# A hybrid RWKV-7 and attention layer: the next block's x fetched and normalised during the running block, and one matrix per chunk and head in the scan

## The chip, the cores and the metric

The kernel runs on one core of one Trainium2 chip. The metric is the device time of one execution in microseconds (us). One execution was also taken by the hardware profiler, which gives the trace that the rows below come from. Engines are named as in the profile: PE (TensorE, matmuls), PEld (its weight loads), DVE (VectorE), ACT (ScalarE), POOL (GpSimd), SP (SyncE, which issues DMAs). Times inside the trace are counted from the start of its span.

## What is computed

One layer on x (2048 tokens of 1024, float32) with three residual steps and a final norm. Half of the first step's width is a recurrent mixer, half a differential attention:

```python
proj = rms_norm(h, norm_mix_w[l]) @ w_in[l]
p_rwkv, p_diff = proj[..., :RWKV_COLS], proj[..., RWKV_COLS:]
h = h + jnp.concatenate([y_rwkv, y_diff], axis=-1) @ w_out[l]
h = h + memory_cross_attn(rms_norm(h, norm_mem_w[l]), rms_norm(mem, norm_src_w[l]), ...)
h = h + jnp.square(jax.nn.relu(hn @ w_up[l])) @ w_down[l]

def step(state, inp):                      # the recurrence, for each of 8 heads of 64
    r_t, w_t, k_t, v_t, kk_t, a_t = inp
    sa = jnp.einsum("bhvk,bhk->bhv", state, -kk_t)
    state = (state * w_t[:, :, None, :] + sa[..., None] * (kk_t * a_t)[:, :, None, :]
             + v_t[..., None] * k_t[:, :, None, :])
    y = jnp.einsum("bhvk,bhk->bhv", state, r_t)
    return state, y
```

The kernel does the recurrence in chunks of 64 tokens: inside a chunk everything is matrix products and the inverse of a triangular matrix, and only a 64x64 state per head goes from chunk to chunk.

## The kernel before

It has two phases. **Phase 1** (0 to about 1424 us) computes the projection `x @ w_in`, the recurrent mixer, the memory's keys and values, and the product with `w_out`. **Phase 2** (the rest: attention queries, memory attention, MLP) is the same in both kernels.

Phase 1 goes over four blocks of 512 tokens. Its backbone is `inproj_stream`, a row of items; an item is one 128x512 output tile made by 24 matmuls (three for each of 8 k-slices, a float32 product split in high and low parts: L631, L632, L634) into a PSUM ring `ps_acc` of two buffers. Its weight pieces come by SP, ACT makes the high part (L615) and POOL the low part (L616). The items' order is lead (2 items), keys, receptances and values of a unit (`rkv`), and `diff` items (q, k, v of the attention half) for each block; after the four blocks come memory items, "fold" items and the `w_out` items (L718 to L738). These matmuls are called the stream.

A unit is one block and one group of four heads (two pairs of heads); there are 8, numbered 0 to 7. Beside the stream each unit goes through a chain: features (`rwkv_features`; its first matmul is L291), scores (`ps_sc`, L359), the transposed scores (`ps_bt` L375, `ps_aT` L384, the latter in 64x64 tiles on the diagonal), the inverse (DVE, with DRAM round trips), the merge (`rwkv_merge`: `psz`, `psr2`, then L500 multiplies the inverse into the matrix `A`), the scan (`rwkv_scan`) and the output (`rwkv_out`). `run()` emits stream matmuls up to a given position, then a step of the unit's generator, and so on: `prep(u+1)` and `finish(u)` run beside each other, both under a raised priority (`urgent`), and the tile scheduler decides from this, from priorities and from its own idea of when data is there, which instruction comes next on each engine. PE takes its instructions in that fixed order.

In the scan a chunk of one pair takes four products of two heads each: L524 (`psu`, from `A` and the column block `UV`, which holds state and v), L526 (`psy`, from `AR`), then, when ACT has copied `psu` into `UV` (L528) and scaled the old state (L521), L534 (`pss`, the new state) and L536 (`psy`, the second part). DVE makes the next state from `pss` (L542). A float32 matmul shows as two records in the trace.

At the start of blocks 1 to 3 the lead item calls `prep_x`: it loads x again by 8 DMAs, transposes it (32 transposes of 128x128, L247), stores the transposed x, multiplies by the norm and splits high and low part; the buffers `xhi` and `xlo` have one copy each. At the start of the memory items `prep_mem` does the same for the memory tokens. At the end of phase 1, `first_queries` puts the first attention queries among the last stream items.

## Time and profile before

| | |
|---|---|
| time, median of 3 runs | 3764.45 us (3763.79 to 3769.11) |
| the profiled execution | 3768.81 us, its span 3767.1 us |
| PE busy | 3581.6 us, 95% |
| DVE, ACT, POOL busy | 1957.9, 1720.5, 1464.5 us |
| mean granted clock of PE | 0.968 |

The page puts 95% of the span as PE busy. A matmul's record covers its way through the array, so that records in a row overlap, and a short matmul that stands alone counts as busy for longer than it holds the next one up. The distance from the start of one record to the start of the next is therefore what the prediction goes by, not the mean length. The granted clock is 1.0 at 2.4 GHz and 0.5 at 1.2 GHz; a value between is a mean of stretches at either.

### The profile page before, as it was taken

The numbers are of one execution on the slowest core, as the hardware profiler recorded it, in microseconds if no ns is written. First come the engines' busy times: TensorE is split into PE (matmuls) and PEld (weight loads), VectorE is DVE, ScalarE is ACT, GpSimd is POOL, SyncE is SP. The second block draws the span as 40 slices with busy tenths as digits, with TensorE's granted clock in tenths as the row PEclk, the third lists the DMA queues.
The fourth block names the chain that finished last, engine by engine and source line by source line (L and its number), as shares of the span: only waits on it lengthen the run. The fifth ranks groups of instructions, "written<-read, shape, count | busy, mean of one in ns | idle before, by whom it ended". The sixth has DMA issues, their size and how long they took to land. (4 is left out here: it accounts for less than half of the span.)

```text
span 3767.1 us, 57886 instructions
## 1 busy us (share of the span) xinstructions
PE 3581.6 (95%) x21297; PEld 2871.5 (76%) x21297; DVE 1957.9 (52%) x4093; ACT 1720.5 (46%) x3802; POOL 1464.5 (39%) x1195
## 2 busy tenths in 40 slices
PE   7999999999999878899999989999999999999998
PEld 5767766767777767678787777888878888888887
DVE  4456666666574636465566756666634332313132
ACT  5364464454455626554455765555543421212123
POOL 4424324423434534344435435343353332222225
PEclk9989999999999899999999999999999999999999
DMA  4343342333335674343324425232243331111113
GB/s 149 107 128 88 82 127 84 86 107 88 87 88 160 207 210 142 106 121 93 113 79 118 139 73 144 79 112 78 85 152 94 111 102 48 48 51 48 48 57 108
DMA packets 566066, 390.52 MB, mean 104 GB/s; under 512 B 65187, under 2 KB 491254, under 8 KB 565782
## 3 DMA queue, kind: packets, MB, share of 16 engines
q1 hardware_dynamic: 534134, 329.55, 30.5%
q10 hardware_dynamic: 28064, 50.35, 4.0%
q0 software_dynamic: 3584, 6.92, 0.8%
q8 instruction: 168, 2.75, 0.3%
q14 instruction: 116, 0.95, 0.1%
HBM read 311.14 MB, written 75.56 MB: 103 GB/s over the span
## 5 line engine op out<-in xcount | busy, mean ns | idle before, releaser
L170 POOL TENSOR_TENSOR wlo<-wraw,whi 128x512 fp32r<-128x512 f32 x520 | 689.5, 1327 | 1247.6 <-ACT whi L169 1218.6
L616 POOL TENSOR_TENSOR wlo<-wraw,whi 128x512 fp32r<-128x512 f32 x288 | 413.8, 1438 | 597.4 <-ACT whi L615 479.3
L169 ACT ACTIVATE whi<-wraw 128x512 fp32r<-128x512 f32 x520 | 327.9, 631 | 639.9 <-PE ps_dn L187 327.0
L186 PE MATMUL ps_dn<-hdh,whi 128*128 128x512 f32 x1024 | 402.1, 393 | 2.3 <-DVE t L1408 1.2
L187 PE MATMUL ps_dn<-hdl,whi 128*128 128x512 f32 x1024 | 401.8, 393 | 0.3 <-DVE hdl L1413 0.3
L188 PE MATMUL ps_dn<-hdh,wlo 128*128 128x512 f32 x1024 | 398.8, 393 | 3.3 <-POOL wlo L170 3.1
L186 PE MATMUL ps_up<-h2h,whi 128*128 128x512 f32 x1024 | 400.1, 391 | 1.0 <-DVE t L1408 0.9
L187 PE MATMUL ps_up<-h2l,whi 128*128 128x512 f32 x1024 | 400.7, 391 | 0.0
L188 PE MATMUL ps_up<-h2h,wlo 128*128 128x512 f32 x1024 | 395.3, 391 | 0.8 <-POOL wlo L170 0.8
L631 PE MATMUL ps_acc<-xhi,whi 128*128 128x512 f32 x832 | 343.7, 414 | 20.0 <-ACT carry L278 18.9
L634 PE MATMUL ps_acc<-xhi,wlo 128*128 128x512 f32 x832 | 343.8, 414 | 2.2 <-POOL wlo L616 2.0
L632 PE MATMUL ps_acc<-xlo,whi 128*128 128x512 f32 x832 | 340.3, 409 | 0.0
L615 ACT ACTIVATE whi<-wraw 128x512 fp32r<-128x512 f32 x288 | 181.2, 630 | 273.4 <-PE ps_acc L632 98.0
L1422 DVE TENSOR_TENSOR ht<-ht,ps_dn 128x512 f32<-128x512 f32 x128 | 87.8, 686 | 347.3 <-PE ps_dn L188 347.2
L1048 ACT ACTIVATE pt<-ps_s,nmx 128x512 f32<-128x512 f32 (+3 forms) x320 | 198.4, 621 | 142.4 <-DVE nmx L1047 117.9
L1047 DVE TENSOR_REDUCE nmx<-ps_s 128x1 f32<-128x512 f32 (+3 forms) x320 | 192.5, 606 | 75.6 <-PE ps_s L1044 71.6
L188 PEld LDWEIGHTS ps_dn<-hdh,wlo 128*128 128x128 f32 x1024 | 193.1, 189 | 45.3 <-POOL wlo L170 6.4
L186 PEld LDWEIGHTS ps_dn<-hdh,whi 128*128 128x128 f32 x1024 | 193.0, 188 | 41.8 <-issue 1.6
L186 PEld LDWEIGHTS ps_up<-h2h,whi 128*128 128x128 f32 x1024 | 192.1, 188 | 41.3 <-DVE t L1408 1.6
L187 PEld LDWEIGHTS ps_dn<-hdl,whi 128*128 128x128 f32 x1024 | 193.2, 189 | 39.8 <-DVE hdl L1413 0.5
L188 PEld LDWEIGHTS ps_up<-h2h,wlo 128*128 128x128 f32 x1024 | 192.4, 188 | 40.3 <-POOL wlo L170 1.5
L187 PEld LDWEIGHTS ps_up<-h2l,whi 128*128 128x128 f32 x1024 | 192.3, 188 | 38.8
(336 smaller groups left out, 7772.4 us busy)
## 6 DMA issues: line engine op xcount, KB each, us to landing
wraw<-in_w_in_dram SPq DMA_DIRECT2D x208, 256.0 KB
wraw<-in_w_down_dram SPq DMA_DIRECT2D x208, 256.0 KB
wraw<-in_w_up_dram SPq DMA_DIRECT2D x192, 256.0 KB
s_hT<-xt ACTq DMA_DIRECT2D x64, 256.0 KB
wraw<-in_w_out_dram SPq DMA_DIRECT2D x56, 256.0 KB
s_qkvT<-qkv ACTq DMA_DIRECT2D x48, 256.0 KB
wraw<-in_w_mq_dram SPq DMA_DIRECT2D x48, 256.0 KB
wraw<-s_mb SPq DMA_DIRECT2D x48, 256.0 KB
```

The source lines that it names most:

```text
L169: nc.scalar.activation(out=hi, in_=raw, func=AF.Copy)
L170: nc.gpsimd.tensor_tensor(out=lo, in0=raw, in1=f32(hi), op=ALU.subtract)
L186: nc.tensor.matmul(ps, whi(k), ahi(k), start=(k == 0), stop=False)
L187: nc.tensor.matmul(ps, whi(k), alo(k), start=False, stop=False)
L188: nc.tensor.matmul(ps, wlo(k), ahi(k), start=False, stop=(k == nk - 1))
L615: nc.scalar.activation(out=hi, in_=raw, func=AF.Copy)
L616: nc.gpsimd.tensor_tensor(out=lo, in0=raw, in1=f32(hi), op=ALU.subtract)
L631: nc.tensor.matmul(o, hi[:, kk, :], xs[k][0], start=(k == 0), stop=False)
L632: nc.tensor.matmul(o, hi[:, kk, :], xs[k][1], start=False, stop=False)
L634: nc.tensor.matmul(o, lo[:, kk, :], xs[k][0], start=False, stop=last)
L1047: nc.vector.tensor_reduce(out=nmx[:, m, c:c + 1], in_=ps[:, 0:w], axis=AX.X, op=ALU.max, negate=True)
L1048: nc.scalar.activation(out=pt[:, cw(c)], in_=ps[:, 0:w], func=AF.Exp, bias=nmx[:, m, c:c + 1], accum_out=sm[:, m, c:c + 1])
```

## The change

Two things. First, `prep_x` is cut in two. `fetch_x` (load, transposes, store, norm) is a generator of 8 steps, run in front of the items m = 16 to 23 of the block before (one k-slice each), into eight new buffers `xn0` to `xn7`; `split_x` (8 high parts on ACT, 4 low parts on DVE, 4 on POOL) is what stays at the block's start. `prep_mem` moves in front of item m = 16 of block 3. The ring `xsl` has 2 buffers where it had 3. Second, the merge makes, for each chunk and head, one matrix `Q` of 128 rows and 128 columns whose product with the head's half of `UV` gives the chunk's new state before its decay and its y at once. The scan of a chunk and pair is then four matmuls in tiles 128x64 (L552) and two scaled copies on ACT; the merge has, for each half of a pair's chunks, 8 matmuls 64x128 (`psw2`, L512), one ACT copy, 16 matmuls 64x128 (`psm`, L520) and six additions on DVE. Scan work falls by 1024 + 512 (L500) matmuls, and 512 (L552) + 256 (`psw2`) + 512 (`psm`) come in. `y` is copied from PSUM by ACT before `rwkv_out`. Last, `dynamic_dma_scratch_size` is set to 2048. The merge's ten steps stand at 0.70 to 0.88 of a unit's stretch, the five of before at 0.72 to 0.88.

```diff
-def prep_x(g, pool, blk, rstd):
+def fetch_x(g, pool, blk, rstd):
...
     for k in range(KD):
-        xt = pool.tile([P, 4, P], F32, tag="xsl", name="xsl", bufs=3)
+        xt = pool.tile([P, 4, P], F32, tag="xsl", name="xsl", bufs=2)
...
+        xn = pool.tile([P, TB], F32, tag=f"xn{k}", name="xn", bufs=1)
+        nc.vector.scalar_tensor_tensor(out=xn, in0=ps, scalar=g.col("nmix", k), in1=sb, op0=ALU.mult, op1=ALU.mult)
+        out.append(xn)
+        yield out
+
+
+def split_x(g, pool, xns):
...
-        nc.scalar.activation(out=hi, in_=xn, func=AF.Copy)
-        eng = nc.gpsimd if blk == 0 and k % 2 else nc.vector
-        eng.tensor_tensor(out=lo, in0=xn, in1=f32(hi), op=ALU.subtract)
+        nc.scalar.activation(out=hi, in_=xns[k], func=AF.Copy)
+        eng = nc.gpsimd if k % 2 else nc.vector
+        eng.tensor_tensor(out=lo, in0=xns[k], in1=f32(hi), op=ALU.subtract)
...
-        psw = [g.ps_misc.tile([P, NCK, CH], F32, tag="misc", name="psw2") for _ in range(2)]
-        for c in range(NCK):
-            for h in range(2):
-                hs = slice(64 * h, 64 * h + 64)
-                for o in (0, 64):
-                    nc.tensor.matmul(psw[h][o:o + 64, c, :], u.aT[hs, c, o:o + 64], u.T[hs, c, :], start=True, stop=True)
-        for h in range(2):
-            nc.scalar.activation(out=u.A[:, :, h, 0:CH], in_=psw[h], func=AF.Copy)
+        for c4 in range(NCK // 4):
+            cs = slice(4 * c4, 4 * c4 + 4)
+            yield
+            psw = g.ps_misc.tile([P, 4, P], F32, tag="misc", name="psw2")
+            for cc in range(4):
+                for hs in HS2:
+                    nc.tensor.matmul(psw[hs, cc, :], u.T[hs, 4 * c4 + cc, :], u.aT[hs, 4 * c4 + cc, :], start=True, stop=True)
+            nc.scalar.activation(out=u.aT[:, cs, :], in_=psw, func=AF.Copy)
+            yield
+            psm = [g.ps_misc.tile([P, 4, P], F32, tag="misc", name="psm") for _ in range(2)]
+            for cc in range(4):
+                c = 4 * c4 + cc
+                for h, hs in enumerate(HS2):
+                    for o in (0, 64):
+                        nc.tensor.matmul(psm[h][o:o + 64, cc, :], u.aT[hs, c, o:o + 64],
+                                         u.Q[hs, c, 2 * h:2 * h + 2, :].rearrange("p a t -> p (a t)"), start=True, stop=True)
...
+                nc.vector.tensor_tensor(out=q2, in0=psm[h][vs], in1=q2, op=ALU.add)
...
-            for h, hs in enumerate(H):
-                nc.tensor.matmul(psu[hs, :], u.A[:, c, h, 0:64], u.UV[:, c, hs], start=True, stop=True)
-            for h, hs in enumerate(H):
-                nc.tensor.matmul(u.psy[hs, c, :], u.AR[hs, c, 1, :], u.UV[hs, c, hs], start=True, stop=False)
-            for h, hs in enumerate(H):
-                nc.scalar.activation(out=u.UV[hs, c, hs], in_=psu[hs, :], func=AF.Copy)
...
+            for h, hs in enumerate(HS2):
+                for i, os in enumerate(HS2):
+                    nc.tensor.matmul(u.psy[h][os, c, :], u.Q[:, c, 2 * h + i, :], u.UV[:, c, hs], start=True, stop=True)
+            for h, hs in enumerate(HS2):
+                o = g.S[hp][hs, :] if c == NCK - 1 else u.UV[hs, c + 1, hs]
+                nc.scalar.activation(out=o, in_=u.psy[h][hs, c, :], func=AF.Copy, scale=u.EC[hs, c:c + 1])
+            yield
...
-                    st[blk] = [prep_x(g, pool, blk, rst[blk]), None, None]
+                    st[blk] = [split_x(g, pool, xns.pop(blk)), None, None]
...
-                if m == 14 and blk + 1 < NB:
+                if blk + 1 == NB:
+                    if m == 16:
+                        st[NB] = [prep_mem(g, pool)]
+                    return
+                if m == 14:
                     rst[blk + 1] = x_stats(g, pool, blk + 1)
+                if m == 16:
+                    fetch[blk + 1] = fetch_x(g, pool, blk + 1, rst[blk + 1])
+                if 16 <= m < 24:
+                    xns[blk + 1] = next(fetch[blk + 1])
```

The order on PE shows it at three places. The first is PE at the start of block 2, in the order of before (stream matmuls of block 1, then transposes of x, `ps_xt`, in a row with scan, `psu` and `psy`, and scores, `ps_sc`):

```order
L631 MATMUL ps_acc<-xhi,whi 128x512
L632 MATMUL ps_acc<-xlo,whi 128x512
L634 MATMUL ps_acc<-xhi,wlo 128x512
L247 MATMUL ps_xt<-ident,xsl 128x128 [waits Activation_49]
L247 MATMUL ps_xt<-ident,xsl 128x128 x3
L526 MATMUL psy_5226<-UV,AR 64x64 [waits DVE_49]
L524 MATMUL psu<-UV,A 64x64 [waits DVE_49]
L524 MATMUL psu<-UV,A 64x64
L526 MATMUL psy_5226<-UV,AR 64x64
L359 MATMUL ps_sc<-AR,BK 128x128 [waits DVE_49]
L359 MATMUL ps_sc<-AR,BK 128x128 x3
L524 MATMUL psu<-UV,A 64x64 [waits DVE_49]
```

and in the order of after, PE inside block 1 (L649, L650 and L652 are the stream's three lines there):

```order
L649 MATMUL ps_acc<-xhi,whi 128x512
L650 MATMUL ps_acc<-xlo,whi 128x512
L652 MATMUL ps_acc<-xhi,wlo 128x512
L247 MATMUL ps_xt<-ident,xsl 128x128 [waits DMAHW2_49,DVE_49]
L247 MATMUL ps_xt<-ident,xsl 128x128 x3
L649 MATMUL ps_acc<-xhi,whi 128x512 [waits Activation_49]
L650 MATMUL ps_acc<-xlo,whi 128x512
L652 MATMUL ps_acc<-xhi,wlo 128x512 [waits Pool_49]
L649 MATMUL ps_acc<-xhi,whi 128x512
```

The transposes of one k-slice stand between two items, and the next item's first matmul waits for ACT; the stream goes on behind.

The second place is PE in the scan. Before, the first half step of two pairs and the start of the second half in the stretch without stream matmuls (`psy_5226` is pair 0's y, `psy_5227` pair 1's):

```order
L526 MATMUL psy_5226<-UV,AR 64x64 [waits DVE_49]
L524 MATMUL psu<-UV,A 64x64 [waits DVE_49]
L524 MATMUL psu<-UV,A 64x64
L526 MATMUL psy_5226<-UV,AR 64x64
L526 MATMUL psy_5227<-UV,AR 64x64 [waits DVE_49]
L524 MATMUL psu<-UV,A 64x64 [waits DVE_49]
L524 MATMUL psu<-UV,A 64x64
L526 MATMUL psy_5227<-UV,AR 64x64
L247 MATMUL ps_xt<-ident,xsl 128x128 [waits DMAHW3_49,DVE_49,PE_49]
L247 MATMUL ps_xt<-ident,xsl 128x128 x3
L536 MATMUL psy_5226<-UV,A 64x64 [waits Activation_49]
L534 MATMUL pss_6012<-UV,BKt 64x64 [waits Activation_49]
```

After, two chunks of pair 1 with a matmul of the next unit's features between (`psa`); `psy` and `psz` are the results of the pair's two heads:

```order
L552 MATMUL psy_6553<-UV,Q 64x64 [waits Activation_49]
L552 MATMUL psy_6553<-UV,Q 64x64
L552 MATMUL psz_6554<-UV,Q 64x64 [waits Activation_49]
L552 MATMUL psz_6554<-UV,Q 64x64
L308 MATMUL psa<-wad,lwa 128x512 [waits Activation_49]
L552 MATMUL psy_6553<-UV,Q 64x64 [waits Activation_49]
L552 MATMUL psy_6553<-UV,Q 64x64
L552 MATMUL psz_6554<-UV,Q 64x64 [waits Activation_49]
L552 MATMUL psz_6554<-UV,Q 64x64
```

A chunk of one pair was L526, L524, L526 and, behind ACT, L536, L534, L536; it is one group of four L552, whose successor waits for ACT.

The third place is PE in the merge of a later unit (`BK` holds the transposed scores, `T` the inverse). In the order of before, the burst of L500 begins so:

```order
L500 MATMUL psw_4909<-T,BK 64x64 [waits PE_49,Activation_49]
L500 MATMUL psw_4909<-T,BK 64x64
L500 MATMUL psw_4910<-T,BK 64x64 [waits PE_49,Activation_49]
L500 MATMUL psw_4910<-T,BK 64x64
L500 MATMUL psw_4909<-T,BK 64x64 x2
L500 MATMUL psw_4910<-T,BK 64x64 x2
```

and in the order of after a half of a pair's chunks reads so, with scan groups between, in a stretch of 152 matmuls without one of the stream:

```order
L512 MATMUL psw_6344<-BK,T 64x128 [waits PE_49]
L512 MATMUL psw_6344<-BK,T 64x128 x7
L552 MATMUL psy_6551<-UV,Q 64x64 [waits Activation_49]
L552 MATMUL psy_6551<-UV,Q 64x64
L552 MATMUL psz_6552<-UV,Q 64x64 [waits DVE_49]
L552 MATMUL psz_6552<-UV,Q 64x64
L520 MATMUL psm<-Q,BK 64x128 [waits Activation_49]
L520 MATMUL psm<-Q,BK 64x128
L520 MATMUL psm<-Q,BK 64x128 [waits PE_49]
L520 MATMUL psm<-Q,BK 64x128 x10
L552 MATMUL psz_6552<-UV,Q 64x64 [waits Activation_49]
L552 MATMUL psz_6552<-UV,Q 64x64
```

What was one run of 64 records per pair is now two groups of `psw2` and two of `psm`, each of which waits for ACT or for PE, and the whole scan of unit 3 stands around the merge of unit 4 with no stream matmul between.

## Rows read from the trace of the kernel before

**Rows 1.** Stretches: us; busy and count per engine; granted clock; DMA share; GB/s
```profile
200.00:1071.00 871.00, 839.29 (x7180) 612.34 (x7172) 553.16 (x1376) 436.37 (x1062) 312.46 (x272) 0.95 0.34 97
1071.00:1424.00 353.00, 303.55 (x2178) 241.90 (x2176) 183.38 (x497) 173.02 (x426) 145.67 (x118) 0.90 0.59 173
```

**Rows 2.** Waits of PE, 0 to 1424: waiting line, releaser, us in total, times, longest
```profile
PE ps_acc L631 <- DVE xres L738: 20.4, 12, 4.2
PE ps_acc L631 <- ACT carry L278: 18.9, 10, 5.1
```

**Rows 3.** Four stretches without a stream matmul, columns as in Rows 1
```profile
222.50:256.70 34.20, 31.44 (x213) 23.63 (x211) 29.23 (x53) 21.85 (x56) 3.81 (x3) 0.63 0.49 157
510.00:545.60 35.60, 32.59 (x275) 23.15 (x273) 29.89 (x57) 24.32 (x65) 5.40 (x7) 0.85 0.47 145
800.90:826.70 25.80, 21.97 (x231) 15.35 (x229) 17.58 (x37) 19.42 (x48) 4.43 (x6) 0.97 0.67 180
1071.00:1110.70 39.70, 35.65 (x330) 25.02 (x329) 30.31 (x81) 28.22 (x84) 6.34 (x9) 0.80 0.38 95
```

**Rows 4.** PE timeline inside the second such stretch: start, length, form, count, wait
```profile
522.16 0.47 PE L526 MATMUL psy<-UV,AR 64*64 64x64 f32 x2
...
529.97 0.33 PE L526 MATMUL psy<-UV,AR 64*64 64x64 f32 x2
...
531.28 1.09 PE L247 MATMUL ps_xt<-ident,xsl 128*128 128x128 f32 x8
532.30 0.27 PE L536 MATMUL psy<-UV,A 128*64 128x64 f32 x1
...
532.96 1.02 PE L338 MATMUL pss<-sq,h 128*2 128x512 f32 x2
533.91 1.91 PE L359 MATMUL ps_sc<-AR,BK 64*128 64x128 f32 x16
535.75 0.32 PE L526 MATMUL psy<-UV,AR 64*64 64x64 f32 x2
```

**Rows 5.** PE groups of that stretch
```profile
L359 PE MATMUL ps_sc<-AR,BK 64*128 64x128 f32 x64 | 9.9, 316 | 1.5 <-DVE A L362 1.5
L526 PE MATMUL psy<-UV,AR 64*64 64x64 f32 x40 | 5.3, 260 | 0.0
```

**Rows 6.** PE timeline, scan bursts between stream matmuls
```profile
488.99 0.40 PE L632 MATMUL ps_acc<-xlo,whi 128*128 128x512 f32 x1
489.31 0.34 PE L524 MATMUL psu<-UV,A 128*64 128x64 f32 x4
489.58 0.33 PE L526 MATMUL psy<-UV,AR 64*64 64x64 f32 x2
489.83 0.50 PE L634 MATMUL ps_acc<-xhi,wlo 128*128 128x512 f32 x1
...
495.52 0.39 PE L634 MATMUL ps_acc<-xhi,wlo 128*128 128x512 f32 x1
...
496.23 0.50 PE L631 MATMUL ps_acc<-xhi,whi 128*128 128x512 f32 x1
```

**Rows 7.** PE timeline, one burst of L500 between stream matmuls
```profile
615.44 0.39 PE L632 MATMUL ps_acc<-xlo,whi 128*128 128x512 f32 x1
615.76 1.16 PE L500 MATMUL psw<-T,BK 64*64 64x64 f32 x64
616.85 0.50 PE L634 MATMUL ps_acc<-xhi,wlo 128*128 128x512 f32 x1
```

**Rows 8.** PE timeline, diagonal 64x64 tiles of L384
```profile
560.66 0.27 PE L384 MATMUL ps_aT<-ident,AR 64*64 64x64 f32 x2
...
560.89 0.27 PE L384 MATMUL ps_aT<-ident,AR 64*64 64x64 f32 x2
```

**Rows 9.** Stretches from one unit's first L291 to the next, busy and count of L631
```profile
492.36:628.93 136.57, 37.43 (x88) 0.93 0.41 115
628.93:769.10 140.17, 45.76 (x111) 0.98 0.30 84
```

More of the change, by code (lines that the diff above doesn't have):

```diff
@@ L82, in _setup_consts @@
     g.finv = 0.022
-    g.fmg = (0.72,0.76,0.80,0.84,0.88)
+    g.fmg = (0.70,0.72,0.74,0.76,0.78,0.80,0.82,0.84,0.86,0.88)
     g.reset = cp.tile([P, TB], F32, name="reset")
@@ L197, in x_stats @@
         for h in range(2):
-            t = pool.tile([P, TB], F32, tag="xsl", name="xld", bufs=3)
+            t = pool.tile([P, TB], F32, tag="xsl", name="xld", bufs=2)
             r0 = blk * TB + j * P
@@ L250, in prep_x @@
         nc.sync.dma_start(out=g.s.xT[k * P:(k + 1) * P, rows], in_=raw)
+        xn = pool.tile([P, TB], F32, tag=f"xn{k}", name="xn", bufs=1)
[3 more added lines that the diff above has]
+def split_x(g, pool, xns):
+    nc = g.nc
+    out = []
+    for k in range(KD):
         hi = pool.tile([P, TB], F32R, tag=f"xhi{k}", name="xhi", bufs=1)
         lo = pool.tile([P, TB], F32R, tag=f"xlo{k}", name="xlo", bufs=1)
[L253 to L257 removed]
+        nc.scalar.activation(out=hi, in_=xns[k], func=AF.Copy)
+        eng = nc.gpsimd if k % 2 else nc.vector
+        eng.tensor_tensor(out=lo, in0=xns[k], in1=f32(hi), op=ALU.subtract)
         out.append((hi, lo))
@@ L351, in rwkv_scores @@
     NCK = TB // CH
-    u.A = up.tile([P, NCK, 2, P], F32, tag="A", name="A", bufs=4)
+    u.Q = up.tile([P, NCK, 4, CH], F32, tag="A", name="Q", bufs=4)
+    u.Lx = g.uq.tile([P, NCK, CH], F32, tag="L", name="L")
     for c4 in range(NCK // 4):
@@ L507, in rwkv_scan @@
     NCK = TB // CH
-    H = (slice(0, 64), slice(64, 128))
     for p in range(2):
         u, hp = us[p], pairs[p]
-        for hs in H:
+        for hs in HS2:
             nc.scalar.activation(out=u.UV[hs, 0, hs], in_=g.S[hp][hs, :], func=AF.Copy)
@@ L529, in rwkv_scan @@
-        yield
-        for p in range(2):
-            u, hp = us[p], pairs[p]
-            pss = g.ps_sm.tile([P, TB], F32, tag=f"sm{p}", name="pss2")[:, 0:CH]
-            for h, hs in enumerate(H):
-                nc.tensor.matmul(pss[hs, :], u.BKt[:, c, hs], u.UV[:, c, hs], start=True, stop=True)
-            for h, hs in enumerate(H):
-                nc.tensor.matmul(u.psy[hs, c, :], u.A[:, c, h, 64:128], u.UV[:, c, hs], start=False, stop=True)
-            if c == NCK - 1:
-                nc.vector.scalar_tensor_tensor(out=g.S[hp], in0=pss, scalar=u.EC[:, c:c + 1], in1=u.se,
-                                               op0=ALU.mult, op1=ALU.add)
-            else:
-                for hs in H:
-                    nc.vector.scalar_tensor_tensor(out=u.UV[hs, c + 1, hs], in0=pss[hs, :], scalar=u.EC[hs, c:c + 1],
-                                                   in1=u.se[hs, :], op0=ALU.mult, op1=ALU.add)
@@ L547, in rwkv_out @@
+    for p in range(2):
+        u = us[p]
+        u.y = up.tile([P, NCK, CH], F32, tag="y", name="y", bufs=2)
+        for h in range(2):
+            nc.scalar.activation(out=u.y[HS2[1 - h]], in_=u.psy[h][HS2[1 - h]], func=AF.Copy)
 def rwkv_out(g, fp, hp, u, gd, blk, pt):
@@ L552, in rwkv_out @@
     mean = g.small.tile([P, NCK], F32, tag="meany", name="meany")
-    nc.vector.tensor_reduce(out=mean, in_=u.psy, axis=AX.X, op=ALU.add)
+    y = u.y
+    nc.vector.tensor_reduce(out=mean, in_=y, axis=AX.X, op=ALU.add)
     nc.vector.tensor_scalar(out=mean, in0=mean, scalar1=-1.0 / 64, scalar2=None, op0=ALU.mult)
-    y = fp.tile([P, NCK, CH], F32, bufs=2, tag="th", name="y")
-    nc.vector.tensor_tensor(out=y, in0=u.psy, in1=mean[:, :, None].to_broadcast([P, NCK, CH]), op=ALU.add)
+    nc.vector.tensor_tensor(out=y, in0=y, in1=mean[:, :, None].to_broadcast([P, NCK, CH]), op=ALU.add)
     yield
@@ L568, in rwkv_out @@
     for c in range(NCK):
-        for hs in (slice(0, 64), slice(64, 128)):
-            nc.tensor.matmul(psb[hs, c * CH:(c + 1) * CH], y[hs, c, :], g.ident[hs, hs], start=True, stop=True)
+        for h, hs in enumerate(HS2):
+            vs = HS2[1 - h]
+            nc.tensor.matmul(psb[hs, c * CH:(c + 1) * CH], y[vs, c, :], g.ident[vs, vs], start=True, stop=True)
     yo = fp.tile([P, TB], F32, bufs=2, tag="th", name="yo")
@@ L641, in prep_mem @@
     nc = g.nc
-    hs = [pool.tile([P, 2, MEMT], F32R, tag=f"xhi{k}", name="mh", bufs=1) for k in range(4)]
-    ls = [pool.tile([P, 2, MEMT], F32R, tag=f"xlo{k}", name="ml", bufs=1) for k in range(4)]
+    hs = [pool.tile([P, 2, MEMT], F32R, tag=f"xn{k}", name="mh", bufs=1) for k in range(4)]
+    ls = [pool.tile([P, 2, MEMT], F32R, tag=f"xn{k + 4}", name="ml", bufs=1) for k in range(4)]
     mh = lambda k: hs[k // 2][:, k % 2, :]
@@ L704, in mem_items @@
     kv = [Item(blk, (g.i.w_mk if m < 8 else g.i.w_mv)[0, :, (m % 8) * P:(m % 8 + 1) * P], post(m),
-               None if m else pre, MEMT) for m in range(16)]
+               None, MEMT) for m in range(16)]
     fold = [Item(blk, g.i.w_mo[0, h * 256:(h + 1) * 256, hf * TB:(hf + 1) * TB], fold_post(h, hf), vt=lambda h=h: vts[h])
@@ L773, in phase1 @@
             g.S.append(s)
-        st, rst, rkvs = {}, {}, {}
+        st, rst, rkvs, xns, fetch = {}, {}, {}, {}, {}
         w_in = lambda m: g.i.w_in[0, :, m * P:(m + 1) * P]
```

48 lines of the change are left out of this document (26 added, 22 removed).

## The prediction

> **What bounds the kernel now.** I read the table of stretches first. From 200 to 1071 us, where the four blocks are computed, PE is busy 839 of 871 us, and all other engines much less [rows 1]; phase 2, from 1424 us on, is not touched. So only the first 1424 us can move, and there the question is what holds the next PE instruction up. The list of waits says that waits alone are small: an item's first matmul waited 18.9 us in all behind ACT's copy that frees the PSUM buffer, and 20.4 us behind the addition of the residual, at the `w_out` items [rows 2]. The loss lies inside "busy". The table of four stretches shows it: at the start of blocks 1, 2 and 3 and of the memory items there are 34.2, 35.6, 25.8 and 39.7 us in which no stream matmul runs, with 213 to 330 records on PE [rows 3]. The timeline inside the second shows short matmuls with distances that come from DVE and ACT [rows 4], and the groups of that stretch a wait behind DVE, 1.5 us [rows 5].
>
> How much of these 135.3 us is needed anyway? The second stretch has 64 `ps_sc` records, which follow each other at 115 ns (16 from 533.91 to 535.75): 7.4 us. It has 160 scan records (four groups of 40): for two pairs a first half takes 1.31 us (529.97 to 531.28) and a second half 0.66 (532.30 to 532.96), that is 1.97 for 32 records or 61 ns each: 9.9 us. It has 32 transposes of x at 128 ns (8 from 531.28 to 532.30): 4.1 us. The 19 left, at about 0.25 us (a 512-column record takes 0.475, two from 532.96 to 533.91; the others are shorter): some 4.5 us [rows 3 to 5]. That is 26 of 35.6 us, 0.095 us per record. At this price the other three need 20, 22 and 31 us, all four 99.5. **36 us** are lost.
>
> **The change part by part.** All is summed on PE, whose order is fixed.
>
> *The boundary.* In the new order items follow each other across the blocks' starts, with the transposes between items, so the loss at the four places goes: −36 us. It goes no further than that, since the transposes and the rest stay. Above, if the loss only moves, it is 0; that is a term of its own, below.
>
> *Fetching.* 24 times a k-slice stands between items, and it uses the `ps_acc` ring, so that the next item's first matmul waits for a copy on ACT that otherwise would be out of the way. The nearest row is that wait before: 18.9 us in 10 waits, 1.9 us each [rows 2]. The floor is 0, the ceiling 24 × 1.9 = 45 us. I take 0.5 us each, since the copy itself is one ACT pass and begins when the transposes are done: **+12**. The loads of x go through SP, at a DMA share of 0.34 in this stretch [rows 1]; I cost them at nothing, because a whole item (24 × 0.23 us) lies ahead of each. *The split* at three block starts: POOL's mean operation is 1.15 us (312.46 us for 272) [rows 1], four of them lie on the first item's path beside ACT's eight; PE uses one k-slice in 0.69 us, so the split nearly keeps pace: about 1.7 us each, **+5** (0 to 14, where four POOL passes show in full).
>
> *The scan.* There are 8 units × 8 chunks × 2 pairs = 128 pair-chunks. Between stream matmuls, six records of the first half stretch the stream from 488.99 to 489.83, 0.84 us where two stream matmuls are 0.23 apart: 0.61, or 0.81 for all eight; the second half's eight take 0.71 − 0.23 = 0.48 [rows 6]. So 1.29 us in the stream, 0.98 in the stretches without [rows 4]. About 40 pair-chunks lie in the latter (10 in the second, by its 40 L526 records at four each [rows 5]): 40 × 0.98 + 88 × 1.29 = 153 us. After: eight records in 128x64 tiles, of the same form and number as that second half: 0.48 × 128 = 61 us. The bounds are 0.33 (the second half in the stretch without stream) and 0.81 (the first half), 42 to 104 us. **−92** (−49 to −111). On ACT 512 copies and scalings become some 256; ACT is half idle, so I count nothing for it.
>
> *The merge.* A burst of L500 goes: it held the stream from 615.44 to 616.85, 1.41 − 0.23 = 1.18 us for 64 records, 16 bursts: −19 us [rows 7]. `psm` comes in: 1024 records in the same four 64x64 tiles, with 128 columns for 64. Twice L500's 18.4 ns is 37: +38, and some 2 us for coming in and out. Floor 18.4 ns: 19; ceiling the 115 ns of `ps_sc`, the same 128 columns where nothing overlaps: 118. `psw2`: 512 records in the two diagonal tiles, 128 columns. The nearest rows are the diagonal tiles of L384, eight records (those left out counted) from 560.66 to 560.89, 29 ns at 64 columns [rows 8]; doubled 58: +30. Floor 29 ns: 15; ceiling 115: 59. Together **+51** (+15 to +158). I take the values that scale with the columns, because both rows have the very tile positions of the new lines.
>
> A rule speaks against that price for `psw2`. Its two tiles write the upper and lower half of one PSUM buffer. The Trainium skill, "TensorEngine Tiling (Array Packing)", Restrictions and Gotchas, says that different row tiles can't access the same PSUM bank at the same time. L384 writes one buffer from two row tiles too, and its 29 ns speak against it here; by the rule the sum would be some 29 us worse. The third rival, below, is that case.
>
> *New stops.* The order shows that the stream stops elsewhere: in the second half of blocks 2 and 3 it waits for a unit's `r` and `k` buffers (two per kind), and there 152 other matmuls stand in a row twice: 64 of the scan (16 pair-chunks, 7.7 us), 24 `psw2` (2.8), 48 `psm` (3.6), 4 of the features (8 records at 0.475, 3.8) and 12 `ps_sc` (24 records, 2.8): 20.7 us of work. In the stretches of before the loss was 36 to 99.5 of work; at that rate each loses 7.5 us, 15 for both. A third, of 62 matmuls, loses 3, and the memory's preparation, which still stands in a row, what it lost before, 39.7 − 31 = 8.7. **+27** (0 if other work fills them, 87 in the fourth rival's case).
>
> *The chain and the end.* A unit's chain gets longer where L500 becomes four rounds of PE, ACT, PE, DVE, shorter by a half step in each of 8 chunks, and DVE is rid of 224 small operations beside the inverse. In the new order the last unit's features come 183 stream matmuls later, its scan is shorter, and about half of the first queries' work falls behind the last stream matmul, where before it filled the waits of the `w_out` items. The stretch from 1071 to 1424 is only 303.55 of 353 us busy at a DMA share of 0.59 [rows 1]. What the end keeps of the gain I can't sum; I take **+5** (−10, since more of the transfers start early, to +25).
>
> Sum: −36 + 12 + 5 − 92 + 51 + 27 + 5 = **−28 us**. Against the profiled execution, 3768.8, that is 3740.8; it was 4.4 above the median of the runs, so 3736 on the median.
>
> **Rivals.**
> 1. *All of it comes.* The merge at its floor (34 − 19 = +15, 36 better), the stops filled but for the memory's (18 better), fetching at half (6 better): −88, **3676**. For it: `psm` has four tiles and long runs. Against: the new stops stand in the order.
> 2. *The chain sets the pace.* From one unit's first L291 to the next are 136.6 us where a stretch without stream lies between, and 140.2 us where none does, while 88 and 111 first-line matmuls fit beside [rows 9]. If the chain's length decides, PE work and stretches count for nothing, and the longer merge pays for the shorter scan: **3764**. Against it: PE is busy 96% of 200 to 1071 [rows 1] and hardly waits for the chain; the period may be equal by the way `run()` deals out the stream.
> 3. *Row tiles take turns.* `psw2` at 115 ns a record: 59 for 30 us, −28 + 29 = +1, **3765**.
> 4. *Slower: the links of the scan lie bare in the new stops.* In the second stretch of before a chunk took 7.8 and 5.8 us (522.16, 529.97, 535.75) [rows 4], where PE's own work for it is 2. My rate makes a stop 28 us for 8 chunks, 3.5 each. If a chunk takes 6.8 there too, a stop lasts 54, 26 more, twice; the shorter ones give 8 more: −28 + 60 = +32, **3796**. A stretch like this also falls to 1.2 GHz: the first one's granted clock was 0.63, a mean of 0.5 and 1.0 [rows 3]. It decides above 5.2 us a chunk. Against it: a chunk has one matmul group and one wait for ACT now, not two and a third for DVE.
>
> **How the numbers follow.** The forecast 0.48, rival 1 0.22, rivals 2 and 3 together 0.12, rival 4 0.18. The likeliest is my sum, 3736; its own range, from the terms' bounds added as independent errors (some 45 us, the merge's ceiling above all), is 3695 to 3775. To hold 8 in 10 the range reaches to rivals 1 and 4: 3675 to 3792. A measurement of this kernel tells about 0.2%, 7.5 us, from no change. Below 3757: forecast and rival 1, 0.70; within: 0.12; above 3772: 0.18.
>
> **What would show it.** Right, if no stretch of 25 us without stream matmuls is left at the blocks' starts, if a group of eight L552 records stretches the stream by about 0.5 us, `psm` follows at 37 and `psw2` at 58 ns, and the stream stops for about 28 us before the rkv items of units 5 and 7. Wrong, if `psw2` or `psm` come at 100 ns or above, if the clock falls in the new stops and a chunk takes over 5 us there, if the fetch items wait over 1 us each behind ACT, or if units still begin 139 us apart although PE has less to do. What gains in the blocks but is lost after the last stream matmul would show in a longer rest of phase 1, from the last `w_out` item to the first matmul of phase 2.

## The result: slower by 2.2%, and phase 1 is longer by 91 us

The changed kernel takes 3851.47 us (median of 4 runs, 3851.04 to 3857.02), the kernel before 3766.78 in the same comparison: the ratio is 1.0223, with an interval from 1.0203 to 1.0242. The forecast was 28 us faster, its range ended at 3792. It came out 85 us slower, and 59 us above the range.

The profiled execution took 3851.04 us, its span is 3849.3. Its stretches, with the columns of [rows 1]:

```profile
200.00:1071.00 871.00, 766.82 (x6217) 561.42 (x6216) 519.95 (x1245) 376.85 (x840) 309.03 (x267) 0.93 0.31 89
1448.00:1514.50 66.50, 49.25 (x206) 37.82 (x204) 45.65 (x160) 38.55 (x104) 13.35 (x13) 0.69 0.26 81
1514.50:3849.00 2334.50, 2255.15 (x10869) 1875.32 (x10869) 1120.08 (x1977) 1013.48 (x2106) 912.03 (x694) 0.99 0.32 95
```

Phase 2 begins at 1514.5 us and takes 2335 us; it began at 1423.3 and took 2344. So phase 1 is 91 us longer. (Phase 2 takes 2332 to 2350 us in the sixteen traces of this document, so that single profiled runs can differ there by more than 10 us.) In the blocks PE is busy 767 us of 871, where [rows 1] had 839: it stands idle 72 us more than before. And there is a stretch of 66 us between the last stream matmul and phase 2, at a granted clock of 0.69, that the kernel before hardly had (8 us). The PE timeline of the kernel before shows its last merge and the first matmul of phase 2:

```profile
1180.91 0.79 PE L500 MATMUL psw<-T,BK 64*64 64x64 f32 x18
...
1423.27 1.16 PE L186 MATMUL ps_wo<-yh,whi 128*128 128x512 f32 x2
```

and the same of the changed kernel, with the last stream matmul and two of the first queries' between:

```profile
1338.55 0.43 PE L520 MATMUL psm<-Q,BK 64*64 64x128 f32 x2
...
1448.09 0.40 PE L652 MATMUL ps_acc<-yhi,wlo 128*128 128x512 f32 x1
...
1450.43 0.50 PE L1068 MATMUL ps_s<-ks,qa 128*128 128x512 f32 x1 [0.79 <-DVE xres L753]
...
1508.04 0.66 PE L158 MATMUL psb<-ident,rstdo 128*128 128x128 f32 x2 [2.63 <-DVE rstdo L1156]
1514.52 0.73 PE L186 MATMUL ps_wo<-yh,whi 128*128 128x512 f32 x2 [1.11 <-ACT yh L1246]
```

The last merge is 157 us later (its last matmul starts at 1338.7, before at 1181.5), the last stream matmul 33 us (1415.1 to 1448.1), phase 2 91 us. Work that stands behind the last merge (the last scan, the last `w_out` items, the first queries) was spread over 242 us of stream before; now it has 176 us to the start of phase 2.

What PE waits for in phase 1, in the columns of [rows 2]:

```profile
PE ps_acc L649 <- ACT carry L286: 20.3, 12, 5.0
PE psy L552 <- ACT UV L555: 17.3, 14, 2.2
PE ps_sc L368 <- DVE BK L331: 14.6, 4, 5.5
PE ps_acc L649 <- ACT qkv L847: 12.3, 6, 3.9
...
PE ps_acc L649 <- DVE xres L753: 4.7, 3, 3.5
```

The wait behind the residual's addition, 20.4 us in [rows 2], has shrunk to 4.7. New are 17.3 us of the scan behind ACT and 14.6 of the scores behind DVE: waits of a unit's chain.

The distances from one unit's features to the next, as in [rows 9], for two units:

```profile
573.50:718.60 145.10, 41.40 (x98) 0.96 0.33 92
718.60:874.20 155.60, 46.22 (x111) 0.92 0.30 82
```

They were 137 and 140. Over units 1 to 7 the mean distance went from 139.4 (212.5 to 1048.7, six distances) to 154.0 us (251.6 to 1175.7), and unit 0's stretch, from its first features matmul to the next unit's, from 158.6 to 199.6.

### The profile page after: what moved, and what is told of

Same layout as the page of the kernel before. It is cut to its first block, busy times and chain, and to the rows that moved or that the text cites. A ratio compares the mean times of both kernels' runs of the same rounds, so it can differ in the third digit from the quotient of the medians.

```text
span 3849.3 us, 56453 instructions
## 1 busy us (share of the span) xinstructions
PE 3577.6 (93%) x20785; PEld 2862.9 (74%) x20785; DVE 1989.4 (52%) x4097; ACT 1677.1 (44%) x3578; POOL 1484.9 (39%) x1207
## 5 line engine op out<-in xcount | busy, mean ns | idle before, releaser
L649 PE MATMUL ps_acc<-xhi,whi 128*128 128x512 f32 x832 | 350.1, 422 | 35.8 <-ACT carry L286 20.3
L652 PE MATMUL ps_acc<-xhi,wlo 128*128 128x512 f32 x832 | 342.6, 412 | 3.2 <-POOL wlo L634 3.2
L650 PE MATMUL ps_acc<-xlo,whi 128*128 128x512 f32 x832 | 340.3, 409 | 0.6 <-POOL xlo L265 0.6
L649 PEld LDWEIGHTS ps_acc<-xhi,whi 128*128 128x128 f32 x832 | 163.5, 196 | 88.5 <-ACT carry L286 24.9
```

The lines of the kernel that those rows point to most:

```text
L649: nc.tensor.matmul(o, hi[:, kk, :], xs[k][0], start=(k == 0), stop=False)
L650: nc.tensor.matmul(o, hi[:, kk, :], xs[k][1], start=False, stop=False)
L652: nc.tensor.matmul(o, lo[:, kk, :], xs[k][0], start=False, stop=last)
```

## What the experiments tested

Two theories stood against each other. **Theory C, the chain:** features, scores, inverse and merge of a unit follow one another, and the next unit's features come only behind the merge; the eight chains in a row set when the last scan, the last `w_out` items and the first queries can run, and the merge has made each of them longer. **Theory P, PE's account:** what counts is PE's work and its stops, as the prediction summed them.

| kernel | last merge ends, us | profiled run, us | ratio to before, interval |
|---|---|---|---|
| psmy_shortinv | 1137.3 | 3745.9 | one run |
| before_shortinv | 1149.4 | 3748.2 | one run |
| before | 1181.5 | 3768.8 | |
| two_f23 | 1183.9 | 3762.0 | 0.9990 (0.9976 to 1.0004) |
| matrix_psmy | 1187.2 | 3772.9 | 1.0008 (0.9994 to 1.0022) |
| fetch_f23 | 1190.1 | 3761.5 | 1.0000 (0.9983 to 1.0016) |
| psmy_two | 1197.7 | 3767.4 | 1.0007 (0.9996 to 1.0018) |
| after_psmy | 1204.1 | 3772.9 | 1.0014 (1.0002 to 1.0026) |
| fetch_only | 1212.4 | 3792.0 | 1.0042 (1.0026 to 1.0059) |
| before_delay | 1238.3 | 3796.1 | one run |
| after_noadd | 1295.5 | 3828.7 | one run |
| after_two | 1303.8 | 3834.4 | one run |
| matrix_only | 1306.9 | 3858.0 | 1.0220 (1.0200 to 1.0239) |
| after | 1338.7 | 3851.0 | 1.0223 (1.0203 to 1.0242) |

The second column is the start of the last `psm` (or L500) matmul in each trace. The two columns rise together but for some 10 us of scatter, whatever was edited: about half a microsecond of total for each microsecond of the last merge ((3851.0 − 3748.2) / (1338.7 − 1149.4) = 0.54). matrix_only, some 20 us above that line, is the one that leaves it most. Some of the scatter is phase 2's, which is the same work but for what is left of the first queries.

### Each half alone

fetch_only has `fetch_x` and `split_x` and all that belongs to them, with the scan and merge of before:

```diff
-                    st[blk] = [prep_x(g, pool, blk, rst[blk]), None, None]
+                    if blk == 0:
+                        xns[0] = list(fetch_x(g, pool, 0, rst[0]))[-1]
+                    st[blk] = [split_x(g, pool, xns.pop(blk)), None, None]
```

> The first half of the change alone: x fetched and normalised in the block before, scan and merge as before. Theory C (the chain of the eight units sets the time: features, scores, inverse and merge of a unit follow one another and the next unit's features come 2 to 5 us behind the merge, and the first queries can only begin behind the last merge): the distance from one unit's first features matmul to the next stays at 137 to 142 us, the last merge ends at 1175 to 1190 us (before 1182, after 1339), and the total is within 12 us of before, 3755 to 3778. Theory P (PE's own account, as in the prediction: the 36 us at the blocks' starts come back, 17 us of waits are paid): 3740 to 3755, and units begin closer together.

Measured: 3789.62 against 3770.79 us, ratio 1.0042 (1.0026 to 1.0059): 0.4% slower, which neither theory had said. The units' distances stay at 140.9 us on average (unit 1 at 225, unit 7 at 1070), as C has it; but unit 1 begins at 225 where it began at 212, and the last merge ends 31 us late, 22 us past the range that C gave. The three stops at the starts of blocks 1 to 3 are gone; the stop of the memory's preparation has moved into block 3, with the columns of [rows 3]:

```profile
922.20:955.20 33.00, 29.72 (x267) 20.01 (x265) 23.94 (x60) 22.98 (x69) 1.89 (x2) 0.64 0.14 41
```

Nothing of the 36 us has come back in the total.

matrix_only has the new scores, merge, scan and output with `prep_x` as before:

```diff
-    u.A = up.tile([P, NCK, 2, P], F32, tag="A", name="A", bufs=4)
+    u.Q = up.tile([P, NCK, 4, CH], F32, tag="A", name="Q", bufs=4)
+    u.Lx = g.uq.tile([P, NCK, CH], F32, tag="L", name="L")
```

> The second half of the change alone: one matrix per chunk and head, blocks' starts as before. Theory C: the merge takes 35 to 40 us where it took 8, units begin about 156 us apart, the last merge ends at 1310 to 1345 us and the total is 3825 to 3865, all of the loss. Theory P (PE has 41 us less work, the loss of the full change comes from stops and waits that seamless starts bring with them): 3730 to 3770.

Measured: 3854.06 us, ratio 1.0220 (1.0200 to 1.0239): the whole loss is in the matrix, as C said. The units begin 150 us apart (247 to 1145).

### A longer chain without any PE work

before_delay puts 16 small copies into the chain of the kernel before:

```diff
+    u = us[0]
+    dl = lp.tile([P, CH], F32, tag="dl", name="dl")
+    for i in range(8):
+        nc.vector.tensor_copy(out=dl, in_=u.T[:, 0, :])
+        nc.scalar.activation(out=u.T[:, 0, :], in_=dl, func=AF.Copy)
     for u in us:
         yield
         psw = [g.ps_misc.tile([P, NCK, CH], F32, tag="misc", name="psw2") for _ in range(2)]
```

> The kernel before with 16 small copies (128x64) in a row, DVE and ACT in turn, between the inverse's merge and L500 of each unit; they give PE no work and their values change nothing. Theory C: the chain gets longer by the row's length, some 12 to 18 us a unit, so that the last merge ends 95 to 145 us later than 1182 and the total is 45 to 90 us above before, 3810 to 3855. Theory P: PE's work is the same and the copies lie beside the stream, at most 15 us more, 3765 to 3782.

Measured: 3796.14 us in one run against 3770.79, 25 us slower and between the ranges of the two theories. The timeline of unit 1's merge shows the first and the last copies and the first L500 (L505 here) behind them:

```profile
341.78 0.19 DVE L496 COPY dl<-T 128x64 f32<-128x64 f32 x1
342.51 0.25 ACT L497 ACTIVATE T<-dl 128x64 f32<-128x64 f32 x1
...
348.77 0.26 ACT L497 ACTIVATE T<-dl 128x64 f32<-128x64 f32 x1
352.84 1.02 PEld L505 LDWEIGHTS psw<-T,BK 64*64 64x64 f32 x64 [0.35 <-ACT qkv L827]
```

The row of copies is 7.3 us long, not the 12 to 18 that I had put; the last merge ended 57 us late, 7.1 us for each of eight units. So nearly every microsecond put into the chain came out at the end of the eight, and not quite half of it in the total. PE got no work, and the total went past the 15 us that theory P allowed at most.

### A shorter chain

after_noadd leaves out the six additions behind `psm` and scales the state by 0, so that the recurrence isn't in the result; the matmuls stay:

```diff
             for h, hs in enumerate(HS2):
...
-                nc.vector.tensor_tensor(out=q2, in0=psm[h][vs], in1=q2, op=ALU.add)
...
-                nc.scalar.activation(out=o, in_=u.psy[h][hs, c, :], func=AF.Copy, scale=u.EC[hs, c:c + 1])
+                nc.scalar.activation(out=o, in_=u.psy[h][hs, c, :], func=AF.Copy, scale=0.0)
```

> The changed kernel without the six additions on DVE behind psm and with the state scaled by 0 (so the recurrence is left out of the result); all matmuls and ACT copies stay, so PE's work is the same. The additions are 3.0 us of each of four rounds of a unit's merge. Theory C: the chain is about 12 us shorter in each unit, the last merge ends near 1245 us instead of 1339, the total is 3785 to 3810. Theory P: PE has the same work and the same stops, 3835 to 3852.

Measured: 3828.66 us, the last merge at 1295.5: 22 us less in total, 43 at the merge. PE has the same matmuls. Both ranges are missed in this one run, P's by 6 us and C's by 19: C had the direction, and twice the size (5 us less a unit at the merge's end, not 12).

after_two puts both `psw2` groups of a pair, with their copies, ahead of its `psm` groups:

```diff
             nc.scalar.activation(out=u.aT[:, cs, :], in_=psw, func=AF.Copy)
+        for c4 in range(NCK // 4):
+            cs = slice(4 * c4, 4 * c4 + 4)
             yield
             psm = [g.ps_misc.tile([P, 4, P], F32, tag="misc", name="psm") for _ in range(2)]
```

> The changed kernel with the merge's two psw2 groups of a pair, and their ACT copies, both ahead of its two psm groups: the same instructions, and in each pair one turn of the ring less in the row. Theory C: 4 to 8 us less a unit, the last merge ends 30 to 65 us earlier than 1339, the total is 3810 to 3840. Theory P: 3845 to 3855.

Measured: 3834.44 us in one run, the last merge at 1303.8, 35 us earlier: as C said, with the very same instructions.

after_psmy gives `psm` other PSUM buffers, and that is all:

```diff
-            psm = [g.ps_misc.tile([P, 4, P], F32, tag="misc", name="psm") for _ in range(2)]
+            psm = [g.ps_y.tile([P, 4, P], F32, tag=f"y{h}", name="psm") for h in range(2)]
```

> The changed kernel with one edit: psm takes the two PSUM buffers y0 and y1, which the scan has left by then, where it took the ring of two that psw2, the features and the scores share. The same instructions in all; a round of the merge need not wait for the additions of the last, and the next unit's features need not wait for any. Theory C (the chain, serial by that ring): units begin 130 to 140 us apart, the last merge ends at 1130 to 1190 us where it ended at 1339, the total is 3690 to 3760, under both kernels. Theory P (PE's account): the stops in which whole scans stand go too, since the order has none of 152 matmuls left, so 16 us come back: 3825 to 3845.

Measured: 3773.66 against 3771.54 us, ratio 1.0014 (1.0002 to 1.0026). Of 85 us of loss, the choice of two idle buffers gives back all but 5. C had said more: the distances came as it said, but the last merge (1204) and the total lie 14 us above its ranges. The distances between units in its trace, from unit 4 to unit 7's features:

```profile
636.30:771.50 135.20, 41.29 (x99) 0.96 0.37 105
771.50:908.50 137.00, 45.62 (x107) 0.96 0.31 84
908.50:1045.80 137.30, 36.32 (x87) 0.86 0.27 75
```

They are like those of the kernel before. Its PE timeline around one merge shows why:

```profile
484.05 1.10 PE L520 MATMUL psm<-Q,BK 64*64 64x128 f32 x32
...
484.98 1.93 PE L512 MATMUL psw<-BK,T 64*64 64x128 f32 x32
...
488.87 1.09 PE L520 MATMUL psm<-Q,BK 64*64 64x128 f32 x16
...
491.18 1.98 PE L299 MATMUL psw<-wad,lwa 64*128 64x512 f32 x4
...
496.51 1.10 PE L520 MATMUL psm<-Q,BK 64*64 64x128 f32 x30
```

The next unit's features (L299, 491.18) start while the second pair's `psm` still has to come (496.51). So the features of a unit need no longer come behind the whole merge of the last. In the changed kernel they stand behind the last addition, below.

before_shortinv goes the other way: 46 of the 108 DVE steps of the inverse are left out of the kernel before, so its inverse is not the whole one:

```diff
-    for i, _ in enumerate(ginter(steps(24, 32, tmp), 62, steps(0, 24, tmp2), 46)):
+    for i, _ in enumerate(steps(24, 32, tmp)):
```

> The kernel before with 46 of the inverse's 108 DVE steps left out (so the inverse is not the whole inverse); all PE work stays. Theory C (the chain bounds the kernel before too): 8 to 14 us less a unit, the last merge ends at 1070 to 1120 us, the total is 3705 to 3750. Theory P (PE's own work and stops bound the kernel before): 3755 to 3770.

Measured: 3748.22 in one run against 3768.43 us (its 19 runs are 3762 to 3783). The row of L500 has its last start at 1149.4 where it was 1181.5:

```profile
L500 PE MATMUL psw<-T,BK x1024: 218/218/365, 197.8 to 1149.4; 64*64 64x64 f32 x171
```

That is 4 us less a unit, half of the least that I had put, and 20 us in the total. Of these, 14 are in phase 1, which ends at 1409.7 where it ended at 1423.3; the other 7 lie in phase 2, where nothing was changed. PE's work is the same as before, and phase 1 is shorter, so the chain bounded it already, at 95% busy.

psmy_shortinv does the same to after_psmy (the same edit).

> The changed kernel with psm in y0 and y1 and with the same 46 steps of the inverse left out. Theory C: as far under the same kernel with the whole inverse (3773) as the kernel before without them is under before, 3705 to 3750, and if PE comes to be what bounds both, the smaller PE work of the new scan shows: 10 to 30 us under the kernel before without those steps. Theory P: 3755 to 3770.

Measured: 3745.88 us, 2 us under before_shortinv. The total hides a difference, though. These are the phases 2 of before_shortinv and psmy_shortinv, with the columns of [rows 1]:

```profile
1409.70:3746.50 2336.80, 2257.59 (x10921) 1878.74 (x10920) 1138.29 (x2027) 1023.61 (x2141) 912.57 (x693) 0.99 0.32 94
1395.10:3744.20 2349.10, 2268.38 (x10922) 1886.96 (x10921) 1135.53 (x2027) 1022.78 (x2142) 910.56 (x693) 0.98 0.32 94
```

In phase 1, where the two differ, psmy_shortinv is 15 us shorter; phase 2, the same work in both, took 12 us longer, at a granted clock of 0.98 where the other had 0.99. So the 10 to 30 us that I had put on less PE work are neither shown nor refuted by one run of each.

### What the last merge holds up

before_noq and after_noq leave out the first queries (the part of the attention for the first 512 tokens is zero), here in the one and the other:

```diff
-    n = 4 * d_steps(1, [0])
-    for i, _ in enumerate(d_stream(g, d, 1, [0])):
-        yield g.fq * i / n
+    z = d.pp.tile([P, TB], F32, tag="ob", name="ob", bufs=1)
+    g.nc.vector.memset(z, 0.0)
+    for h in range(4):
+        g.nc.sync.dma_start(out=g.s.oT[h * P:(h + 1) * P, 0:TB], in_=z)
+        yield g.fq * h / 4
```

> The kernel before without the first queries at the end of phase 1 (their output is set to zero, that part of the attention is left out). Theory C: the w_out items are bound by transfers there, phase 2 starts at 1395 to 1425 us, total 3735 to 3768.

> The changed kernel without the first queries (their output is set to zero, that part of the attention is left out). Theory C: what the late chain costs is mostly that the first queries begin behind the last merge and run on when the stream has ended, so that without them phase 2 starts at 1425 to 1455 us, and the distance to the kernel before without them is 20 to 45 us, not 85. Theory P (PE's stops and waits in the blocks make the loss): the distance stays at 70 to 90 us.

Measured, in one run each: 3743.83 and 3801.62 us; phase 2 begins at 1394.5 and 1458.6 us. The distance is 58 us, between what the two theories said: the queries make 27 of the 85 us, and 58 stay without them. There the last stream matmul itself is late, 1448.2 against 1387.8. The `w_out` items of the last block need the last unit's output (its last `psb` starts at 1388.7 in the changed kernel, 1255.6 before), so the late chain, as I read it, holds the stream's own end. I had put too much on the queries.

### Why the early fetch brings nothing

matrix_psmy is matrix_only with `psm` in y0 and y1 (the edit of after_psmy), so after_psmy without the fetch.

> The matrix per chunk and head alone, blocks' starts as before, with psm in y0 and y1. If the early fetch is worth nothing while the chain sets the pace: 3765 to 3780, as with the fetch (3773). If the early fetch pays as soon as the merge is short: 15 to 35 us above that, 3785 to 3805. If the fetch costs by its waits, as it seemed to do alone: 3745 to 3765.

Measured: ratio 1.0008 (0.9994 to 1.0022), the first of the three cases: with the fetch 1.0014, without it 1.0008, not to be told apart. psmy_two has the edits of after_psmy and after_two together.

> The changed kernel with psm in y0 and y1 and both psw2 groups of a pair ahead of its psm groups: the same instructions. Theory C: the next unit's features can begin 2 to 5 us earlier in each unit, last merge 1170 to 1200 us, total 3745 to 3770. If the chain is no longer what bounds it: 3770 to 3778.

Measured: 3768.24 against 3768.43 us, ratio 1.0007 (0.9996 to 1.0018); the last merge at 1197.7, 6 us earlier. Level with before.

In fetch_only 13 of the 22 us by which unit 7 begins late are there when unit 1 begins, behind the first block. The list of waits there, from 50 to 225 us (waiting line, releaser, us in total, times, longest):

```profile
PE ps_acc L639 <- ACT carry L286: 4.2, 1, 4.2
PE ps_acc L639 <- ACT qkv L837: 3.0, 1, 3.0
```

The kernel before waits 0.3 us for these two in that stretch. fetch_f23 and two_f23 fetch early for blocks 2 and 3 only, the one with the old scan, the other as psmy_two:

```diff
-                    if blk == 0:
-                        xns[0] = list(fetch_x(g, pool, 0, rst[0]))[-1]
+                    if blk < 2:
+                        xns[blk] = list(fetch_x(g, pool, blk, rst[blk]))[-1]
...
-                if 16 <= m < 24:
+                if 16 <= m < 24 and blk:
```

> The early fetch alone (old scan and merge), and only for blocks 2 and 3; block 1's x and its transposes are done at its start, as in the kernel before. Open is where the fetch alone loses some 15 us. If it is the first block (its units begin 12 us later from unit 1 on, and the distances after that are as before): 3768 to 3778, the same as before within its error. If each fetched block costs its share: 3778 to 3786. If the early fetch pays where the chain of the first unit isn't held up: 3745 to 3763.

> The changed kernel with psm in y0 and y1, both psw2 groups of a pair ahead of its psm groups, and the early fetch only for blocks 2 and 3. If the first block's fetch costs what is missing: unit 1 begins near 212 us where it began at 220, the last merge ends at 1180 to 1192, the total is 3755 to 3765, under before. If not: 3765 to 3775, level with before.

Measured: 3765.31 against 3764.33 us, ratio 1.0000 (0.9983 to 1.0016), and 3761.07 against 3764.33, ratio 0.9990 (0.9976 to 1.0004). Without the first block's early fetch the loss of fetch_only is gone (the smaller `xsl` ring is in fetch_f23 too, so it isn't that), and the other blocks' fetch is worth nothing that shows. The story of unit 1 is only half true: in two_f23 it begins at 210 us and the last merge ends at 1183.9, but in fetch_f23 it begins at 219, later than before, and the time is still that of before. No version that computes the whole result was measurably faster than the kernel before.

## Why the prediction was wrong, by its own steps

**The step that failed is "the chain and the end", +5 us (−10 to +25), together with rival 2.** I had seen the chain of 139 us, and saw from the rows that it was the same with a stop of the stream and without [rows 9]; I put that down, as a possibility, to `run()`, wrote that "the longer merge pays for the shorter scan", and gave it 3764 us and, with another rival, 0.12. In place of these 5 us phase 1 came out 91 us longer, and nothing of the other terms' gain showed. Both halves of the sentence are off. The scan isn't in the chain that the next unit waits for, so a shorter scan pays for nothing there. And the merge was sized by its PE work. Before, a unit's two bursts of L500 begin at 615.76 [rows 7], and the next features at 628.93 [rows 9]: 13 us. In the changed kernel, PE in unit 2's merge:

```profile
533.97 0.39 PE L649 MATMUL ps_acc<-xhi,whi 128*128 128x512 f32 x1
534.29 1.09 PE L512 MATMUL psw<-BK,T 64*64 64x128 f32 x16
535.31 0.50 PE L649 MATMUL ps_acc<-xhi,whi 128*128 128x512 f32 x1
...
538.84 0.39 PE L650 MATMUL ps_acc<-xlo,whi 128*128 128x512 f32 x1
539.16 1.10 PE L520 MATMUL psm<-Q,BK 64*64 64x128 f32 x32
540.19 0.50 PE L652 MATMUL ps_acc<-xhi,wlo 128*128 128x512 f32 x1
```

and all engines from there to the next features, in the same merge:

```profile
537.14 0.60 ACT L513 ACTIVATE BK<-psw 128x512 f32<-128x512 f32 x1
...
540.30 0.69 DVE L527 TENSOR_TENSOR Q<-psm,Q 64x512 f32<-64x512 f32 x1 [8.08 <-PE psm L520]
...
542.71 0.42 DVE L530 TENSOR_TENSOR Q<-psm,AR 64x256 f32<-64x256 f32 x1
...
562.88 0.87 PE L512 MATMUL psw<-BK,T 64*64 64x128 f32 x10
...
567.09 0.87 PE L520 MATMUL psm<-Q,BK 64*64 64x128 f32 x20
...
570.24 0.42 DVE L530 TENSOR_TENSOR Q<-psm,AR 64x256 f32<-64x256 f32 x1
...
573.54 1.12 PE L299 MATMUL psw<-wad,lwa 64*128 64x512 f32 x2
```

One round: `psw2` at 534.29, ACT's copy at 537.14, `psm` at 539.16, six additions on DVE from 540.30 to 543.1. The fourth `psw2` ends near 563.8, the last additions at 570.7, the features of unit 3 start at 573.54. That is 39 us from the first `psw2` to the features, 26 more than before (in the units whose merge falls into a stop it is 27 us, 691.9 to 718.6 in unit 3). The features came that late because their PSUM buffer is of the ring of two (`misc`) that `psm` held: in unit 3's merge, below, PE is seen to wait for the last addition with the next features (718.57), and in after_psmy, which frees them of it, 80 of the 85 us are gone.

The means over units 1 to 6 add up the same way. From the first merge matmul to the next features it was 13 us before, 39 in the changed kernel and 13 in after_psmy; from a unit's features to its first merge matmul 126, 115 and 125. So 26 us came in and 11 came back ahead of the merge, which leaves the 15 us by which the units lie farther apart. Why 11 come back isn't tested; the shorter scan isn't the reason, since after_psmy has it too.

**The terms of PE were about right, and their gain didn't show.** A group of eight L552 records, in the changed kernel:

```profile
557.19 0.40 PE L650 MATMUL ps_acc<-xlo,whi 128*128 128x512 f32 x1
557.52 0.34 PE L552 MATMUL psz<-UV,Q 128*64 128x64 f32 x4
557.69 0.29 PE L552 MATMUL psy<-UV,Q 128*64 128x64 f32 x4
557.90 0.50 PE L652 MATMUL ps_acc<-xhi,wlo 128*128 128x512 f32 x1
```

It stretched the stream by 0.71 − 0.23 = 0.48 us, as I had put. `psm` stretched the stream by 1.35 − 0.23 = 1.12 us for 32 records, 35 ns each where I took 37; `psw2` by 1.34 − 0.23 = 1.11 for 16, 69 ns where I took 58. So the row tiles of `psw2` do overlap in one PSUM buffer, less than I took. The rule of rival 3 (the Trainium skill, "TensorEngine Tiling (Array Packing)", Restrictions and Gotchas) would have made it 115 here and doesn't hold in this trace as it is written. The merge and scan together did give PE less work, but the 72 us of [rows 1]'s stretch are waiting and not that: over all of phase 1 PE is busy 1319 us before, 1322 in the changed kernel and 1288 in after_psmy. These 31 us less didn't shorten after_psmy, since PE wasn't what the units waited for; with the ring freed, what came is rival 2, no change. "95% busy" in the page was the share of a PE that fills itself with the stream whenever a chain lets it, and before_shortinv shows that it had room.

**The boundary's −36 us didn't come**: fetch_f23 (1.0000) and after_psmy against matrix_psmy show that. The reason, as I read it, is the same: in these stops the chains of two units went on, and what the stream lost there it did not need before the last chain ended. **Fetching, +12**, showed as a cost only in fetch_only, in the first block; why the first block's two waits, 7 us, make 19 us at the end in fetch_only is not settled by these runs.

**The new stops** were in the order and in the trace, and the two long ones were longer than 28 us (the third lasts 26 us, from 411.5):

```profile
701.40:739.80 38.40, 27.73 (x306) 18.71 (x305) 29.10 (x56) 21.76 (x54) 1.27 (x1) 0.75 0.05 15
999.60:1038.50 38.90, 25.94 (x306) 18.23 (x304) 28.26 (x54) 21.72 (x54) 1.27 (x1) 0.82 0.05 15
```

Inside the first the `psw2` groups come 5.4 us apart, one merge round with scan groups but no stream beside it (in unit 2, among the stream, the rounds are 9 to 11 us apart):

```profile
702.03 1.09 PE L512 MATMUL psw<-BK,T 64*64 64x128 f32 x16
...
707.45 1.09 PE L512 MATMUL psw<-BK,T 64*64 64x128 f32 x16
...
712.87 1.09 PE L512 MATMUL psw<-BK,T 64*64 64x128 f32 x16
...
718.57 1.09 PE L299 MATMUL psw<-wad,lwa 64*128 64x512 f32 x2 [0.61 <-DVE Q L530]
```

Three rounds of a merge and then the features make 16.5 us in a row before the stop is half over; the other 21 us, to 739.8, hold the features and scores of unit 4, at a granted clock of 0.55. Rival 4 saw the scan's links bare, but the chunks came 3.3 us apart (eight from 701.8 to 728.3), under its 5.2; the bare links were the merge's, then those of the next unit's features and scores. Rival 4 had the right sign, and the fall of the clock, but by the wrong links.

**The range** was also added up wrongly. The terms' bounds, taken as independent errors, give some 53 us to the fast side and some 140 to the slow one, not 45. Such a range would have held 3851, but by luck: what widens it most are the prices of `psm` and `psw2` on PE and rival 4's stops, not the wait that came.

The sum of what I expected and what came: the predicted gain of 28 us didn't come since neither of its two terms, PE's work and the stops at the starts, was on the path that sets the end; the loss of 85 is what reached the total of the merge's longer round trips in the eight units.

What stays open: how much of the rest of the chain could be taken away before PE's work counts (psmy_shortinv, 4 us shorter in a unit than before_shortinv, may already show some of it in phase 1); why matrix_only lies 20 us above the line of the others; and how much of a merge's length comes from the places at which `run()` deals its ten steps. These places were the same in all versions of the new merge, and in after_psmy, where `psm` has its own buffers, it still takes 22 to 36 us from the first to the last matmul.

## What to carry to other kernels

A busy share of 95% on an engine that runs a filler stream says that the filler is there, not that the engine is the bound: look for a period that stays the same when the filler stops, and test it by lengthening the chain with work for other engines. When a step of a serial chain is replaced, size the new step by its round trips (matmul, copy, matmul, additions) and by the buffers that it holds, not by its matmuls. A buffer ring shared with the next stage ties the two together; a free buffer elsewhere may be worth more than all the matmuls saved.

## What the runs showed of the hardware

Two diagonal 64x64 tiles with 128 columns that write the two halves of one PSUM buffer came at 69 ns a record between stream matmuls, four tiles in two buffers at 35 ns, where the 64x128 tiles of the scores, with the same 128 columns, had come at 115. All three stretches ran at a granted clock of 1.00. Long stretches without the stream ran at a lower granted clock: the 66 us behind the last stream matmul ran at a granted clock of 0.69, the two stops of 38 us at 0.75 and 0.82.
